# The last chunk of a scan turned inside the next output projection, with its product moved to the end

## The chip, the cores and the metric

One core of one Trainium2 chip runs the whole program. The metric is the device time of one execution in microseconds (us). The kernel before takes 3092.04 us, the median of three runs between 3091.47 and 3092.46. The profiler recorded one further execution of 3090.91 us. Engines are called as the profile calls them: PE is TensorE's matrix multiplication, DVE VectorE, ACT ScalarE, POOL GpSimd, SP SyncE, which issues most transfers.

## The reference

A small decoder trunk of two layers over 2048 tokens of width 1024, in float32: a Mamba-2 layer with a chunked scan, then a layer of latent attention whose keys and values come from the stream after the first layer. The change lies in the first layer, of which this is the core:

```python
proj = h @ w_in
z, xBC, dt_raw = jnp.split(proj, [D_INNER, D_INNER + CONV_DIM], axis=-1)
xBC = jax.nn.silu(causal_depthwise_conv(xBC, conv_w, conv_b))
xs, Bm, Cm = jnp.split(xBC, [D_INNER, D_INNER + SSM_GROUPS * SSM_STATE], axis=-1)
dt = jax.nn.softplus((dt_raw + dt_bias).astype(jnp.float32))
y = ssd_chunked_scan(xh, dt, A, Bm, Cm)            # 4 groups, each 8 heads of 64
y = y + D_skip[:, None] * xh
y = y * jax.nn.silu(z)
y = y * lax.rsqrt(jnp.mean(y * y, axis=-1, keepdims=True) + EPS)   # per group of 512
return (y * g_out) @ w_out
```

## The kernel before, in words

**Tiling.** The 2048 tokens are four blocks b of 512, and the 2048 inner columns four groups g of 512. The pair (b, g) is an item; the sixteen items run in order, b outermost. For an item there are four pieces of work. `xbc` and `zgate` are the input projections, matrix products into PSUM banks of the tag "mm", of which there are four. `zgate` ends with its four row tiles, each bank read by ACT (L639, a tanh) and then by DVE (L640) into the tile sz, after which the bank is free. `ssd` is the scan over four chunks of 128 rows. `outp` is the output projection, in two halves n of 512 output columns. Each half is a `sweep` of 16 products: four row tiles i by four column slices k of the inner dimension. A product is three matmuls (L88, L89, L90), of high and low parts of both operands. When a row tile has its four products, DVE adds the bank to the residual rows hs (L719).

**Between scan and projection.** A finished chunk of the scan, y (128 rows by 512), leaves ACT at L900. The projection needs it with the inner dimension on the partitions, so `turn` transposes it: four PE transposes (L812) into a PSUM bank of the tag "tr" (four banks as well), and from there ACT makes the high part and DVE the low part of a tile yT (L119 and L120, for block 0 L111 and L112). Row tile i of `outp` uses the yT of chunk i. The chunks 0 to 2 are turned in the course of the next chunk; chunk 3 is turned in the last but one of the scan's 20 steps.

**Interleaving.** In item (b, g), the program goes through the 8 parts of `outp` of the item before, then the parts of `xbc` and `zgate` of the item after, and takes a step of the scan of (b, g) whenever its share of the 20 is due (the `while` in `mamba`). In the items with g = 2 three further parts come behind them: loading and normalising the next block's rows, transposing them into xT, and `steps(b + 1)`. The last makes the step sizes of the whole next block: 16 matmuls (L733), a copy by ACT (L737), four transposes (L740), twenty-five short DVE instructions in a chain (L755 to L771, a softplus by series), three matmuls for the sums along a chunk (L773 to L775), and from these ACT's and DVE's tiles d_cum, d_dec, d_ecum and d_wend (L777 to L783). `steps(1)`, for example, is emitted at the end of item (0, 2). The following scan (0, 3) still works on block 0 and needs none of its results, but a scan of a later item does.

**Order.** Nothing here is sorted by hand at the level of instructions: the Tile framework sets each engine's order when the program is built, by priorities and by its own estimates of durations. Each engine then runs its list strictly in that order. So the order that the program is emitted in and the order that an engine runs differ, and a change of the source may move other instructions than those it touches.

**A boundary.** Where one item's scan ends and its `outp` begins, PE has the last matmuls of `zgate` of the next item, L812 of the last chunk, and then `outp`'s products. The first instructions of the scan that follows are L834 and L835 (the transposed B and the product CB), then L850 (four transposes of x) and L870 (the products within a chunk). On ACT and DVE, L844, L841, L845 and L853 belong to the same first steps.

Of the kernel before, what the change touches and what calls it, by code (L numbers as in the profile page):

```python
# [71 lines left out]
class Net:  # L72
# [16 lines left out]
        mm(out, l_hi, r_lo, start=False, stop=False)  # L89
        mm(out, l_lo, r_hi, start=False, stop=stop)  # L90

    def sweep(self, nk, banks, weights, product, evacuate):


        ni, w = len(banks), {}
        order = [(k, i) for i in range(ni) for k in (0, 1)]
        order += [(k, i) for k in range(2, nk - 2) for i in range(ni)]
        order += [(k, i) for i in range(ni) for k in (nk - 2, nk - 1)]
        for n, (k, i) in enumerate(order):
            if k not in w:  # L100
                w[k] = weights(k)
            product(banks[i], k, i, w[k], k == 0, k == nk - 1)
            if k == nk - 1:
                evacuate(banks[i], i)
            if n % ni == ni - 1:
                yield
# [233 lines left out]
    def mamba(self, cp):  # L340
        nc = self.nc
        self.state = [None] * G
        self.xn, self.xT, self.dtv, self.conv, self.sz, self.yT, self.rr, self.hs = {}, {}, {}, {}, {}, {}, {}, {}
        items = [(b, g) for b in range(NB) for g in range(G)]
        self.load_x(0, self.a["x"][0:TB])
        self.layer_constants(cp)
        self.held, self.owed = {}, []
        first = [self.t(self.sp, "big", [P, D], bufs=2) for _ in range(2)]
        first += [self.t(self.hh, "hs", [P, D], bufs=4) for _ in range(4)]
        first += [self.t(self.sp, "yT", [P, D], bufs=4) for _ in range(4)]  # L350

        def later(kind):
            return self.t(self.hh, "hx", [P, D], bufs=4)

        def together(*parts):
            for group in zip_longest(*parts):
                yield

        def beneath(part, *others):
            for _ in part:  # L360
                for other in others:
                    next(other, None)
                yield

        def behind(part, n):
            for _ in range(n):
                yield
            yield from part

        hold = self.scan(0, (0,), lambda kind: first.pop(0), True)  # L370
        rest = [self.scan(0, (kind,), lambda kind: first.pop(0), True) for kind in (1, 2)]
        ahead = self.scan(1, (0, 1, 2), later)
        for part in (hold, self.prep(0, self.g0), rest[0], self.steps(0), together(self.xbc(0, 0), rest[1]),
                     together(self.zgate(0, 0), ahead)):
            for _ in part:
                pass
        def thinned(part, n):
            for m, _ in enumerate(part):
                yield
                if m % n == n - 1:  # L380
                    yield

        background = thinned(self.second_weights(), 2)
        for n, (b, g) in enumerate(items):
            parts, total = [], 0
            if n:
                parts.append(self.outp(*items[n - 1]))
                total += 8
            turned = iter(())
            if g == G - 2:  # L390
                self.load_x(b + 1, self.a["x"][(b + 1) * TB:(b + 2) * TB] if b + 1 < NB else self.h_d[0:TB])
                turned = behind(self.prep(b + 1, self.g0 if b + 1 < NB else None, each=1), 2)
            if n + 1 < len(items):
                beside = iter(())
                if b == 0 and g < 2:
                    beside = self.scan(g + 2, (0, 1, 2), later, early=2)
                elif b == 1:
                    beside = thinned(self.out_power(g), 1)
                elif b:
                    beside = background  # L400
                parts += [beneath(self.xbc(*items[n + 1]), beside), beneath(self.zgate(*items[n + 1]), beside, turned)]
                if b < 2 or (b, g) == (NB - 1, G - 2):
                    parts.append(beside)
                total += 24
            else:
                parts.append(self.mla_gate(0, 0))
                total += 8
            if g == G - 2:
                parts.append(turned)
                total += 2  # L410
                if b + 1 < NB:
                    parts.append(self.steps(b + 1))
                    total += 1
            scan, done, step = self.ssd(b, g), 0, 0
            for part in parts:
                for _ in part:
                    step += 1
                    while done * total < 20 * step and done < 20:
                        next(scan, None)
                        done += 1  # L420
            for _ in scan:
                pass
        self.tail = self.outp(*items[-1])
# [274 lines left out]
    def outp(self, b, g):  # L698

        nc, a, t0 = self.nc, self.a, b * TB  # L700
        if g == 0:
            self.hs[b] = [self.t(self.hh, "hs", [P, D], bufs=4) for _ in range(4)]
            for i in range(4):
                nc.sync.dma_start(self.hs[b][i], a["x"][t0 + i * P:t0 + (i + 1) * P, :])
        hs, yT, rr = self.hs[b], self.yT.pop((b, g)), self.rr.pop((b, g))
        for n in range(2):
            banks = [self.t(self.pp, "mm", [P, TB], bufs=4) for _ in range(4)]

            made = {}

            def weights(j):
                return self.w_out(b, g, n, j, made)

            def product(bank, j, i, w, start, stop):
                self.mm3(bank, yT[i][:, 0, j, :], yT[i][:, 1, j, :], *w, start, stop)

            def evacuate(bank, i):
                hv = hs[i][:, n * 512:(n + 1) * 512]
                nc.vector.scalar_tensor_tensor(hv, bank, rr[:, i:i + 1], hv, ALU.mult, ALU.add)  # L719

            yield from self.sweep(4, banks, weights, product, evacuate)
        if g == G - 1:
            for i in range(4):
                nc.sync.dma_start(self.h_d[t0 + i * P:t0 + (i + 1) * P, :], hs[i])
# [64 lines left out]
    def ssd(self, b, g):  # L789
# [3 lines left out]
        BT, CT, *xs = self.conv.pop((b, g))  # L793
        szs = self.sz.pop((b, g))
        ms, pw = (self.t(self.sm, n, [P, 4]) for n in ("ms", "pw"))
        self.yT[b, g] = []

        def v8(x):
            return x.rearrange("p (h d) -> p h d", h=8)
# [9 lines left out]
        def turn(y):  # L809
            ps = self.t(self.pp, "tr", [P, TB], bufs=4)  # L810
            for j in range(4):
                nc.tensor.transpose(ps[:, j * P:(j + 1) * P], y[:, j * P:(j + 1) * P], self.ident)  # L812
            u = self.t(self.sp, "yT", [P, 2, 4, P], F16 if b else F32R, bufs=4)
            (self.pair16 if b else self.split)(u[:, 0], u[:, 1], ps.rearrange("p (j t) -> p j t", j=4))
            self.yT[b, g].append(u)

        ready = []
        if b:
            old = halves(pair("Sp", TB, 1), self.state[g])
        for c in range(4):  # L820
# [42 lines left out]
            if ready:  # L863
                turn(ready.pop(0))
                yield
# [34 lines left out]
                act(y, y, AF.Copy, scale=pw[:, c:c + 1])  # L900
            yield
            ready.append(y)
        turn(ready.pop(0))
        yield
        r = self.rsqrt(self.sm, ms, 4)
        rr = self.t(self.sm, "rr", [P, 4])
# [613 lines left out]
```

## Time and profile before

| | |
|---|---|
| median of three runs | 3092.04 us |
| the profiled execution | 3090.91 us |
| span from its first to its last instruction | 3088.9 us |
| PE busy | 2995.3 us (97%) |
| DVE busy | 2313.6 us (75%) |
| ACT busy | 1931.2 us (63%) |
| POOL busy | 615.4 us (20%) |
| mean granted PE clock | 0.994 |

The span leaves out 2.0 us of the profiled execution's own time, and the median is 1.1 us above that. The share of busy time is a mean over the whole program, of which the sixteen items are the first half: the last scan step of the items ends at about 1534 us. Names in a row are the program's tile names: `y<-y,pw 128x512` writes 128 partitions by 512 elements of y. A row of the timeline has the start, the duration, the engine, the line, the operation and, in brackets, how long the engine stood idle before it and what released it. Matmuls overlap in the pipeline, so the distance from one start to the next tells the pace, not the duration. A wait that is shown by line and tile is the sum over the program, with the number of times and the longest.

### The profile page before, as it was taken

What the parts mean: (1) busy time and instruction counts of PE and PEld (TensorE: products, weight loads), DVE (VectorE), ACT (ScalarE), POOL (GpSimd) and SP (SyncE); (2) the same over time, 40 slices, a digit from 0 to 9 for tenths busy, and PEclk for the clock granted to TensorE, in tenths of its full rate; (3) what the DMA queues carried; (4) which work ended last, traced back from release to release, by engine and by line L of the source; (5) the groups of instructions that cost most, each with busy time, mean ns of one, the idle gap of its engine ahead of it and who ended that gap; (6) DMA issues with size and microseconds to landing.
All of it is one profiled execution on the core that took longest, in us unless ns stands there. A gap on an engine that the chain in (4) does not pass through costs nothing.

```text
span 3088.9 us, 51063 instructions
## 1 busy us (share of the span) xinstructions
PE 2995.3 (97%) x17758; PEld 1760.5 (57%) x17758; DVE 2313.6 (75%) x5034; ACT 1931.2 (63%) x4920; POOL 615.4 (20%) x842
## 2 busy tenths in 40 slices
PE   7899999999999999999999999999999999999998
PEld 3466655545455554545555455466666666665777
DVE  6789887778777787887755544488888888888676
ACT  8777566655666665565534333278888888888522
POOL 0212122211212112222111211422222222222100
PEclk9999999999999999999999999999999999999999
DMA  8675436354455366354466555622323223232494
GB/s 287 225 242 184 146 105 218 127 169 152 147 203 163 131 194 217 133 195 150 147 206 205 184 184 163 195 67 53 68 54 66 53 54 65 54 87 76 126 270 153
DMA packets 205064, 457.09 MB, mean 148 GB/s; under 512 B 28115, under 2 KB 57555, under 8 KB 203365
## 3 DMA queue, kind: packets, MB, share of 16 engines
q1 hardware_dynamic: 176948, 375.94, 38.0%
q0 software_dynamic: 27856, 77.89, 9.8%
q8 instruction: 140, 2.29, 0.3%
q14 instruction: 120, 0.97, 0.1%
HBM read 340.99 MB, written 112.73 MB: 147 GB/s over the span
## 4 chain that ended last, share of the span: by engine, by line
PE 36%; ACT 6%; DVE 6%; issue 4%; DMA 2%; POOL 0%; SPq 0%; ACTq 0%; POOLq 0%; DVEq 0%
PE mm L88 6%; PE mm L90 6%; PE mm L89 6%; PE tr L1254 5%; PE tr L88 3%; ACT Pr L1236 3%; PE tr L89 3%; PE tr L90 3%; PE tr L1264 2%; PE tr L1265 2%; ACT PTs L119 2%; DVE PTs L120 1%; DVE mx L1228 1%; DMA os<-ri_d 1%; DMA wr<-in_mla_w_out_dram 0%
## 5 line engine op out<-in xcount | busy, mean ns | idle before, releaser
L120 DVE SCALAR_TENSOR_TENSOR PTs<-tr,PTs 128x512 f16<-128x512 f32 (+3 forms) x640 | 376.8, 607 | 99.2 <-ACT PTs L119 92.7
L1236 ACT ACTIVATE Pr<-mm,nm 128x512 f32<-128x512 f32 (+2 forms) x631 | 397.5, 638 | 21.7 <-DVE nm L1231 21.5
L119 ACT ACTIVATE PTs<-tr 128x512 f16<-128x512 f32 (+3 forms) x640 | 331.3, 541 | 121.0 <-PE tr L1254 111.5
L1228 DVE TENSOR_REDUCE mx<-mm 128x1 f32<-128x512 f32 (+2 forms) x569 | 338.9, 617 | 31.4 <-PE mm L90 26.7
L1254 PE MATMUL tr<-pack,Pr 128*128 128x128 f32 x2176 | 320.4, 273 | 3.4 <-DVE PTs L120 2.4
L88 PE MATMUL mm<-xT,wsp 128*128 128x512 f16 x800 | 305.7, 382 | 7.6 <-ACT wsp L119 4.6
L89 PE MATMUL mm<-xT,wsp 128*128 128x512 f16 x800 | 304.9, 381 | 0.0
L90 PE MATMUL mm<-xT,wsp 128*128 128x512 f16 x800 | 304.5, 381 | 0.0
L1254 PEld LDWEIGHTS tr<-pack,Pr 128*128 128x128 f32 x2176 | 253.3, 141 | 76.0 <-PE mm L1223 6.7
L88 PE MATMUL mm<-K,xT 96*128 96x512 f16 (+2 forms) x639 | 222.5, 348 | 16.8 <-ACT Pr L1236 14.1
L88 PE MATMUL mm<-wsp,xT 128*128 128x512 f16 (+1 forms) x640 | 232.2, 364 | 4.5 <-ACT craw L610 4.3
L89 PE MATMUL mm<-wsp,xT 128*128 128x512 f16 (+1 forms) x640 | 232.3, 363 | 3.2 <-DVE wsp L120 3.2
L616 DVE SCALAR_TENSOR_TENSOR cacc<-craw,pack,cacc 128x512 f32<-128x512 f32 x288 | 219.5, 791 | 17.6 <-ACT cacc L614 17.0
L90 PE MATMUL mm<-wsp,xT 128*128 128x512 f16 (+1 forms) x640 | 232.1, 363 | 0.0
L89 PEld LDWEIGHTS <-xT 128*128 128x128 f16 (+1 forms) x1408 | 138.1, 98 | 152.1 <-issue 43.2
L1264 PE MATMUL tr<-PTs,xT 128*128 128x512 f16 (+3 forms) x640 | 221.0, 347 | 1.7 <-ACT Os L1271 1.3
L90 PE MATMUL mm<-K,xT 96*128 96x512 f16 (+2 forms) x639 | 221.8, 347 | 0.0
L89 PE MATMUL mm<-K,xT 96*128 96x512 f16 (+2 forms) x639 | 221.2, 346 | 0.0
L1265 PE MATMUL tr<-PTs,xT 128*128 128x512 f16 (+3 forms) x640 | 219.2, 347 | 0.0
L90 PEld LDWEIGHTS <-xT 128*128 128x128 f16 (+1 forms) x1408 | 137.0, 97 | 133.1 <-issue 5.5
L88 PEld LDWEIGHTS <-xT 128*128 128x128 f16 (+1 forms) x1408 | 137.6, 98 | 120.1 <-issue 8.5
L88 PE MATMUL mm<-wsp,yT 128*128 128x512 f16 (+1 forms) x512 | 197.4, 385 | 1.2 <-DVE sz L640 1.0
(458 smaller groups left out, 6796.0 us busy)
## 6 DMA issues: line engine op xcount, KB each, us to landing
wsp<-wi_d SPq DMA_DIRECT2D x96, 512.0 KB, 3.7
big<-cumT SPq DMA_DIRECT2D x64, 512.0 KB, 4.8
wraw<-in_ssm_w_out_dram SPq DMA_DIRECT2D x96, 256.0 KB, 3.8
wi_d<-wsp SPq DMA_DIRECT2D x32, 512.0 KB, 3.6
wsp<-wo_d SPq DMA_DIRECT2D x32, 512.0 KB, 3.4
wsp<-wu_d SPq DMA_DIRECT2D x28, 512.0 KB, 3.8
hx<-in_ssm_w_in_dram SPq DMA_DIRECT2D x48, 256.0 KB, 4.4
wraw<-in_ssm_w_in_dram SPq DMA_DIRECT2D x48, 256.0 KB, 4.5
```

Of the source, the lines that this page charges most:

```text
L88: mm(out, l_hi, r_hi, start=start, stop=False)
L89: mm(out, l_hi, r_lo, start=False, stop=False)
L90: mm(out, l_lo, r_hi, start=False, stop=stop)
L119: self.nc.scalar.activation(hi, src, AF.Copy, scale=scale)
L120: self.nc.vector.scalar_tensor_tensor(lo, src, scale, hi, ALU.mult, ALU.subtract)
L616: nc.vector.scalar_tensor_tensor(acc, raw[:, k:k + TB], wk[k], acc, ALU.mult, ALU.add)
L1228: v.tensor_reduce(mx[:, n:n + 1], s[:, :w], AX.X, ALU.max)
L1236: nc.scalar.activation(x[:, :w], s[:, :w], AF.Exp, bias=nm, accum_out=sm[:, j, n:n + 1])
L1254: nc.tensor.transpose(pt[:, j * P:(j + 1) * P], st["P"][j][kb], self.ident)
L1264: nc.tensor.matmul(st["O"][:, c], vals[h][:, kb, :], u[:, 0], start=kb == 0, stop=False)
L1265: nc.tensor.matmul(st["O"][:, c], vals[h][:, kb, :], u[:, 1], start=False, stop=kb == nk - 1)
```

## The change

The last chunk's `turn` is no longer a step of the scan. It is kept in a table `last_turn` and called by `outp`, once, after the first part of its first half: in the order of emission behind four products and behind the next scan's first step. So that the projection has work that does not need the last row tile, the first half's sweep orders its sixteen products differently: those of the row tiles 0 to 2 first, twelve of them, then the four of row tile 3. The second half keeps its order. No instruction is added or removed, and the values are the same.

```diff
-    def sweep(self, nk, banks, weights, product, evacuate):
+    def sweep(self, nk, banks, weights, product, evacuate, waits=False):
...
         order += [(k, i) for i in range(ni) for k in (nk - 2, nk - 1)]
+        if waits:
+            order = [x for x in order if x[1] < ni - 1] + [x for x in order if x[1] == ni - 1]
         for n, (k, i) in enumerate(order):
...
         self.state = [None] * G
+        self.last_turn = {}
...
-            yield from self.sweep(4, banks, weights, product, evacuate)
+            for m, _ in enumerate(self.sweep(4, banks, weights, product, evacuate, n == 0)):
+                yield
+                if n + m == 0:
+                    self.last_turn.pop((b, g))()
...
-        self.yT[b, g] = []
+        rows = self.yT[b, g] = []
...
-            self.yT[b, g].append(u)
+            rows.append(u)
...
-        turn(ready.pop(0))
+        self.last_turn[b, g] = lambda: turn(ready.pop(0))
         yield
```

The lines of the changed file stand a few further down: L812 is L818, L719 is L722, L733 L739, L740 L746, L771 L777, L773 L779, L834 L840, L850 L856, L870 L876, L845 L851, L853 L859, L112 and L120 are L114 and L122, L640 is L643.

PE at the end of item (1, 3), an ordinary boundary (xT are the operands of `zgate`, yT those of `outp`). Before:

```order
L90 LDWEIGHTS xT_8103
L90 MATMUL mm_8957<-wsp_9131,xT_8103 128x512
L812 MATMUL tr_9151<-pack,y_9000 128x128 x4
L88 LDWEIGHTS xT_8095
L88 MATMUL mm_8958<-wsp_9131,xT_8095 128x512
```

Of the change:

```order
L90 LDWEIGHTS yT_8752
L90 MATMUL mm_9197<-wsp_9200,yT_8752 128x512
L840 MATMUL tr_9228<-pack,BC_8637 128x128
L841 MATMUL tr_9228<-BC_8682,BC_8637 128x128
L818 MATMUL tr_9249<-pack,y_9000 128x128 x4
L88 LDWEIGHTS yT_9037
L88 MATMUL mm_9198<-wsp_9200,yT_9037 128x512
```

The turn stood between two products of `zgate`, with twelve more matmuls of `zgate` behind it before the first of `outp`; it now stands behind the first twelve matmuls of `outp` and the first two of the next scan.

PE in the item (1, 2), where `steps(2)` lies (d_... and big_8131 or big_8123 are its tiles). Before, up to the sums along a chunk:

```order
L90 LDWEIGHTS yT_7655
L90 MATMUL mm_8374<-wsp_8377,yT_7655 128x512
L773 MATMUL tr_8166<-big_8131,pack 128x128
L774 MATMUL tr_8166<-big_8131,ones 128x128
L775 MATMUL tr_8166<-pack,big_8131 128x128
L834 MATMUL tr_8242<-pack,BC_7500 128x128
L835 MATMUL tr_8242<-BC_7532,BC_7500 128x128
L850 MATMUL tr_8275<-pack,xs_7737 128x128
```

Of the change:

```order
L90 LDWEIGHTS yT_7974
L90 MATMUL mm_8204<-wsp_8269,yT_7974 128x512
L779 MATMUL tr_8158<-big_8123,pack 128x128
L780 MATMUL tr_8158<-big_8123,ones 128x128
L781 MATMUL tr_8158<-pack,big_8123 128x128
L840 MATMUL tr_8234<-pack,BC_7500 128x128
L841 MATMUL tr_8234<-BC_7532,BC_7500 128x128
L818 MATMUL tr_8255<-pack,y_7907 128x128 x4
L856 MATMUL tr_8286<-pack,xs_7737 128x128
```

The three matmuls L773 to L775 stood in the second half of `outp` (bank mm_8374); they now stand behind the last product of row tile 2 in the first half (bank mm_8204), with L812 behind them. Between the transposes L740 and the first of the three, PE's list has 55, 50 and 64 matmuls in the items (0, 2), (1, 2) and (2, 2) before, and 31, 30 and 30 of the change.

DVE at the same place, the instructions that make the low part of the last chunk's yT. Before, between two other turns:

```order
L120 SCALAR_TENSOR_TENSOR xT_8103<-tr_8098,pack,xT_8103 128x512
L120 SCALAR_TENSOR_TENSOR yT_8111<-tr_8106,yT_8111 128x512
L242 TENSOR_SCALAR rsy_8187<-rsb_8185 128x4
```

Of the change:

```order
L777 TENSOR_TENSOR big_8123<-d_dt_8155,pack 128x128
L786 TENSOR_TENSOR d_wend_8165<-tr_8158,d_cum_8162 128x128
L789 COPY big_8123<-tr_8158 128x128
L114 TENSOR_TENSOR Bt_8237<-tr_8234,Bt_8237 128x128
L788 TENSOR_TENSOR d_wend_8165<-d_wend_8165,d_dt_8155 128x128
L847 TENSOR_TENSOR CB_8243<-tr_8234,pack 128x128
L851 TENSOR_TENSOR big_8232<-big_8232,CB_8243 128x1024
L859 TENSOR_TENSOR Xd_8291<-tr_8286,d_dt_4074 128x512
L122 SCALAR_TENSOR_TENSOR yT_8260<-tr_8255,yT_8260 128x512
```

The low part was made ahead of the steps' chain; it now comes behind the whole chain and behind the first instructions of the next scan (CB, the 128x1024 product, Xd).

## The prediction

> **What bounds the kernel now.** I read the page's busy table first: PE works 2995.3 of 3088.9 us, so a change that leaves PE's instructions alone can move only the 94 us in which it stands, and the time that a lower clock costs it. Then I read what PE waits for at the lines that the change touches.
>
> ```profile
> PE tr L812 <- ACT y L900: 9.8, 7, 3.2
> PE tr L812 <- ACT xT L119: 1.9, 1, 1.9
> PE tr L773 <- DVE big L771: 1.2, 2, 0.7
> PE mm L88 <- DVE sz L640: 1.0, 3, 0.5
> PE tr L812 <- DVE hx L552: 0.9, 1, 0.9
> PE tr L812 <- DVE xT L120: 0.5, 1, 0.5
> ```
>
> The columns are the sum in us, the number of times and the longest. L812 waits 13.1 us in all: 9.8 for the chunk's own y, and 3.3 at the three boundaries beside which the next block's steps lie, for a "tr" bank. That is all that this change can take away directly. L773, in the chain of the steps, and the first matmul of a bank (L88, for sz) wait almost nothing.
>
> Next the granted clock around the wait of the item (1, 1), by windows; the columns are the window, its length, busy time and count of PE, its loads, DVE, ACT and POOL, then the clock, the DMA share and GB/s.
>
> ```profile
> 626.28 0.84 PE L812 MATMUL tr<-pack,y 128*128 128x128 f32 x4 [1.96 <-ACT y L900]
> ```
> ```profile
> 624.30:626.60 2.30, 0.34 (x4) 0.32 (x4) 2.06 (x14) 2.30 (x6) 0.00 (x0) 1.00 0.87 314
> 626.60:630.00 3.40, 3.40 (x12) 1.42 (x10) 2.57 (x13) 3.40 (x8) 0.00 (x0) 0.50 0.75 254
> 630.00:634.00 4.00, 4.00 (x22) 2.01 (x21) 3.90 (x13) 3.36 (x5) 0.00 (x0) 1.00 0.22 68
> ```
>
> After a wait of 1.96 us PE runs 3.4 us at clock 0.50: that doubles its work there, so about 1.7 us are lost behind the wait. The trace has five such stretches behind L812's waits, so up to 13.1 + 8.5 = 21.6 us hang on this instruction. The question is what stands in its place.
>
> **Part 1, an ordinary boundary.** PE's new list has outp's first products where L812 stood. They need a "mm" bank, which is free when DVE has read the last of it into sz (L640), behind ACT's L639. The boundary at (1, 3):
>
> ```profile
> 820.91 0.38 PE L90 MATMUL mm<-wsp,xT 128*128 128x512 f16 x1
> 824.47 1.05 PE L812 MATMUL tr<-pack,y 128*128 128x128 f32 x4 [3.18 <-ACT y L900]
> 825.55 1.24 ACT L639 ACTIVATE sz<-mm,half 128x512 f32<-128x512 f32 x2
> 826.64 0.68 DVE L640 SCALAR_TENSOR_TENSOR sz<-sz,mm 128x512 f32<-128x512 f32 x1
> ```
>
> ACT's list has L639 behind L900, in both orders. Without L812, PE goes on at 820.91 + 0.22 with the last twelve matmuls of zgate at 0.216 each (the pace is worked out in part 2) and reaches outp's first at 823.7. The bank is free at 826.64 + 0.68 = 827.3, and 0.1 later the matmul starts: a wait of 3.7 in place of 3.18. The same working for three others:
>
> ```profile
> 535.76 0.66 PE L812 MATMUL tr<-pack,y 128*128 128x128 f32 x4 [1.34 <-ACT y L900]
> 1195.34 0.66 PE L812 MATMUL tr<-pack,y 128*128 128x128 f32 x4 [2.41 <-ACT y L900]
> ```
> ```profile
> 537.93 0.68 DVE L640 SCALAR_TENSOR_TENSOR sz<-sz,mm 128x512 f32<-128x512 f32 x1
> 629.14 0.68 DVE L640 SCALAR_TENSOR_TENSOR sz<-sz,mm 128x512 f32<-128x512 f32 x1
> 1198.36 0.68 DVE L640 SCALAR_TENSOR_TENSOR sz<-sz,mm 128x512 f32<-128x512 f32 x1
> ```
>
> PE is there at 535.76 - 1.34 + 2.6 = 537.0, 626.9 and 1195.5; the bank is free at 538.7, 629.9 and 1199.1. The waits are 1.7, 3.0 and 3.6 where 1.34, 1.96 and 2.41 stood. The four sum to 12.0 against 8.9: **+3.1**, and the stretches at half clock behind them stay as many. Before, L812's wait covered this one. The rest of L812's 9.8 (0.9, at later boundaries) I let go: **-0.6**. The price lies between -8.9 (the bank is free earlier than the rows say) and +4. That row tile 3 is late costs nothing here: its product stands at least 24 matmuls, 5.2 us, behind its turn, and ACT and DVE need 0.7 us each for yT.
>
> **Part 2, the three boundaries with the next block's steps.** The reorder lets twelve products of outp run early, and the scheduler, which holds the steps' chain to be short, puts L773 to L775 right behind them: 31, 30 and 30 matmuls behind L740 where 55, 50 and 64 stood. L773 needs the end of DVE's chain, and everything on PE queues behind it: the next scan's L834, L835, L812 itself, and the rest of outp. How long the chain takes at (1, 2):
>
> ```profile
> 735.02 0.39 PE L89 MATMUL mm<-wsp,yT 128*128 128x512 f16 x1
> 745.61 0.38 PE L90 MATMUL mm<-wsp,yT 128*128 128x512 f16 x1
> 746.51 0.46 PE L773 MATMUL tr<-big,pack 128*128 128x128 f32 x2 [0.52 <-DVE big L771]
> 748.02 0.38 PE L88 MATMUL mm<-wsp,yT 128*128 128x512 f16 x1
> ```
> ```profile
> 735.13 0.29 DVE L755 TENSOR_TENSOR big<-tr,pack 128x128 f32<-128x128 f32 x1 [3.06 <-PE tr L740]
> 746.07 0.29 DVE L771 TENSOR_TENSOR big<-d_dt,pack 128x128 f32<-128x128 f32 x1
> 749.60 1.22 DVE L845 TENSOR_TENSOR big<-big,CB 128x1024 f32<-128x1024 f32 x1
> ```
>
> The first two rows are the first and last of the 50 matmuls: 49 gaps in 10.59 us, 0.216 each. DVE's chain runs from 735.13 to 746.36, 11.23 us; of the change it holds three evictions of hs where it held four, each 0.66 from start to start like the next fence's conversion: 10.6. L755 starts 0.11 behind the first matmul and L773 0.15 behind the chain's end, so L773 can start 10.9 us after that matmul. PE is there after 30 x 0.216 = 6.5: it waits **4.3** (before, 0.52). At (0, 2) and (2, 2):
>
> ```profile
> 358.73 0.50 PE L88 MATMUL mm<-wsp,yT 128*128 128x512 f32 x1
> 371.11 0.39 PE L88 MATMUL mm<-wsp,yT 128*128 128x512 f32 x1
> ```
> ```profile
> 358.84 0.29 DVE L755 TENSOR_TENSOR big<-tr,pack 128x128 f32<-128x128 f32 x1 [2.17 <-PE tr L740]
> 370.33 0.74 DVE L115 SCALAR_TENSOR_TENSOR wsp<-wraw,pack,wsp 128x512 fp32r<-128x512 f32 x1
> 370.99 0.28 DVE L771 TENSOR_TENSOR big<-d_dt,pack 128x128 f32<-128x128 f32 x1
> ```
> ```profile
> 1104.73 0.29 DVE L755 TENSOR_TENSOR big<-tr,pack 128x128 f32<-128x128 f32 x1 [0.23 <-PE tr L740]
> 1118.12 0.28 DVE L771 TENSOR_TENSOR big<-d_dt,pack 128x128 f32<-128x128 f32 x1
> ```
>
> At (0, 2) the chain takes 12.43, of the change less one eviction and two conversions, 10.5; PE needs 31 x 0.229 = 7.1: a wait of **3.6**. At (2, 2) it takes 13.68, less an eviction and one conversion, 12.35; PE needs 6.5: **6.1**. Together 14.0, less the 0.5 of before: **+13.5**. Bounds: 0.7 for each conversion or eviction that moves, so 11 to 15. L812's 3.3 us here are no gain, since the bank they wait for is now taken by L733, next in the list.
>
> **Part 3, row tile 3 at those boundaries.** The turn comes behind L773, and DVE's half of yT behind the big product L845 and Xd. At (1, 2) L845 ends at 750.82, 4.3 us after L773's start; 0.7 for yT makes 5.0. PE, from L773 to the end of L850, takes 748.02 - 746.51 = 1.5, with 0.44 for L812, seven matmuls (1.5) and nine of L870 (0.3) 3.8 until it needs the low part: a wait of **1.3**, and the same at (0, 2). At (2, 2) ACT has a weight conversion ahead of its half, but a wait of before falls away:
>
> ```profile
> 1119.36 0.72 ACT L119 ACTIVATE wraw<-wraw,gains 128x512 f16<-128x512 f32 x1 [1.95 <-DMA wraw<-in_mla_w_in_dram]
> 1126.10 1.12 PE L870 MATMUL tr<-Xd,big 128*64 128x64 f32 x31 [2.21 <-issue]
> ```
>
> With the conversion 1.3 + 0.7, and up to 4.0 if its transfer is late again; less 2.21, between -0.9 and +4. I take 0. **+2.6** in all.
>
> **Part 4, the clock.** Waits of 1.96 us were followed by one half-clock stretch; three new waits of 3.6 to 6.1 bring one or two each. Four at 1.7 are 6.8; what PE waits in part 3 it would have waited anyway, which covers about 2.3: **+4.5**, between 2.5 and 8.5.
>
> [...]
>
> **Part 5, what is paid back.** Behind the new waits PE has 20 to 34 more matmuls (4.3 to 7.3 us) between L773 and the item's end than before, so the next boundary's wait, at (1, 3) and (2, 3), may shrink. Against it, (1, 0) and (1, 1) wait there too without any steps ahead of them: that wait comes from the chain behind the last chunk. I take **-3**, between 0 and -10.7 (3.7 + 3.6 and two stretches).
>
> **The sum:** 3.1 - 0.6 + 13.5 + 2.6 + 4.5 - 3 = +20.1 on the profiled 3090.9, that is 3111.0; the median lies 1.1 above the profiled execution: **3112 us**. With all costs low and the payback whole it is +7 or so, 3099; with all high, +33, 3125.
>
> **The rivals.** *ACT's list at (2, 3)*, on the far side of the forecast: two conversions of the value weights (L477) now stand ahead of L639.
>
> ```profile
> 1208.74 0.72 ACT L477 ACTIVATE wraw<-wraw,pack 128x512 fp32r<-128x512 f32 x1 [0.67 <-DMA wraw<-in_kv_w_up_dram]
> ```
>
> If their transfer lands as late as it did, tanh waits until 1209.5 where it started about 1197.6; PE lags by up to 8 us by then, so 4 to 12 more: 3116 to 3124. For it: the row's wait for a DMA. Against it: the transfers are issued earlier in the new order. 0.15.
>
> *The banks are free in time* at ordinary boundaries, so that L812's 8.9 us and three stretches (5.1) are gained there, while parts 2 to 4 stand: 20.1 - 2.5 - 14 = +3.6, 3096. Against it, L639 is behind L900 in ACT's list. 0.12.
>
> *Faster:* the wait at L812 is the true bound and L773 finds its chain done. It decides if DVE's chain falls below the 6.5 us that PE needs; then the 13.1 us and five stretches go, less what sz takes: 3070 to 3085. Against it, 10.6 us of instructions in one engine's list. 0.09.
>
> *Nothing measurable:* the payback is whole and the banks are free earlier by a microsecond or two: 3092 to 3098. 0.10.
>
> **The numbers.** The forecast has 0.54, within 3099 to 3125. The range 3094 to 3125 takes in the rivals at 3096 and 3116 to 3124. A measurement tells 0.2%, 6.2 us, from no change. Slower: the forecast, the first rival and some of the second, 0.77; the same: most of the second and the last, 0.13; faster: 0.10.
>
> **What would show it.** Right: PE waits of 4 to 6 us at L773 (now L779) in three places, for DVE's big; L812 (now L818) waits below 1 us in all, while the wait of L88 for sz rises from 1.0 to about 12; clock 0.50 behind the three. Wrong: L88's wait for sz stays small (part 1), L779 waits under 2 us (part 2), or the end waits of (1, 3) and (2, 3) vanish (part 5 was the larger).

## The result, and the profile after

The changed kernel takes 3110.12 us, the median of six runs from 3106.36 to 3120.19; the kernel before, run beside it, 3092.06 us. The ratio is 1.007, with a 95% interval from 1.0059 to 1.0081: slower by 18 to 25 us. The forecast was 3112 us, slower. The profiled execution took 3106.36 us with a span of 3104.4, that is 15.5 more than the span before, and PE is busy 2998.4 us where it was 2995.3. It was the fastest of the six, so an account of this trace explains 15.5 us and leaves the rest of the 18 to 25 open.

What PE waits for in the items of the first layer (the waits between 300 and 1600 us; the columns are the sum, the times and the longest), in the changed kernel:

```profile
PE tr L779 <- DVE big L777: 15.1, 3, 7.2
PE mm L88 <- DVE sz L643: 10.9, 7, 3.6
PE mm L88 <- ACT craw L613: 8.4, 5, 3.3
PE tr L739 <- DVE xT L122: 2.9, 2, 1.8
PE tr L739 <- DVE hx L555: 0.9, 1, 0.9
PE mm L88 <- ACT yT L121: 0.8, 1, 0.8
```

The same view of the kernel before, where it has more than the prediction showed:

```profile
PE mm L88 <- ACT craw L610: 5.9, 4, 3.3
PE tr L870 <- issue: 2.2, 1, 2.2
PE tr L89 <- POOL Xp L806: 1.8, 3, 0.6
PE mm L88 <- DVE hs L719: 1.4, 2, 0.9
PE tr L773 <- DVE big L771: 0.5, 1, 0.5
```

Read the two side by side. The turn (L818) no longer waits at all. The 13.1 us that it waited before are at other instructions: 10.9 at the first matmuls of outp, for sz, and 3.8 at L739 (2.9 + 0.9), which now takes the "tr" bank that the turn took. On top stand 15.1 us at L779, the sums along a chunk of the next block's steps, where 0.5 stood. The three waits of L779, by the timeline of PE:

```profile
372.05 0.46 PE L779 MATMUL tr<-big,pack 128*128 128x128 f32 x2 [3.64 <-DVE big L777]
748.75 0.46 PE L779 MATMUL tr<-big,pack 128*128 128x128 f32 x1 [4.31 <-DVE big L777]
1123.12 0.77 PE L779 MATMUL tr<-big,pack 128*128 128x128 f32 x2 [7.15 <-DVE big L777]
```

They were forecast as 3.6, 4.3 and 6.1. The granted clock around four waits of the changed kernel, by windows (the third number from the right is the clock):

```profile
634.00:638.00 4.00, 2.20 (x11) 0.88 (x9) 3.76 (x20) 4.00 (x8) 0.00 (x0) 1.00 0.96 322
834.00:838.00 4.00, 3.80 (x22) 2.16 (x22) 3.64 (x13) 1.10 (x3) 0.00 (x0) 1.00 0.84 238
1123.00:1130.00 7.00, 6.13 (x27) 4.49 (x27) 4.43 (x10) 3.66 (x10) 0.00 (x0) 0.66 0.80 252
1216.00:1220.00 4.00, 3.94 (x11) 1.49 (x11) 1.80 (x4) 1.03 (x2) 0.00 (x0) 0.57 0.00 0
```

Behind the waits for sz at (1, 1) and (1, 3), 1.80 and 1.86 us long, the clock stays at 1.00; behind the one at (2, 3), 3.62 us long, it falls, and at L779 at (2, 2) it is at 0.50 for two stretches, from 1120.9 to 1127.7 us. Counted in narrow windows up to 1620 us, the trace of before has nine stretches of 3.4 us at half clock and the changed one eleven. In such a stretch the matmuls start 0.43 us apart (before, from 627.34 to 629.48 us) and after it 0.22 (from 630.18 us on), so half of the time that PE worked in the stretches is taken as lost: by this estimate 14.0 us before and 16.4 now, +2.4.

The account by these views: L779 +14.6 (15.1 - 0.5); sz and the turn's y together +0.6 (10.9 - 0.5 - 9.8); craw +2.5; the bank before the steps +0.5 (3.8 - 3.3); row tile 3 and the wait in its place -1.4 (0.8 - 2.2); Xp and hs, for which PE no longer waits, -3.2 (1.8 + 1.4); the clock +2.4. That is +16.0 against 15.5 of the span; small waits that the views above leave out, and those of the second layer, are not in it.

### The profile page after: what moved, and what is told of

The parts are those of the page before. It is cut to its first block, busy times and chain, and to the rows that moved or that the text cites. A ratio compares the mean times of both kernels' runs of the same rounds, so it can differ in the third digit from the quotient of the medians.

```text
span 3104.4 us, 51077 instructions
## 1 busy us (share of the span) xinstructions
PE 2998.4 (97%) x17758; PEld 1763.8 (57%) x17758; DVE 2315.5 (75%) x5034; ACT 1930.9 (62%) x4920; POOL 614.9 (20%) x842
## 4 chain that ended last, share of the span: by engine, by line
PE 57%; DVE 14%; ACT 9%; DMA 5%; issue 5%; POOL 1%; SPq 0%; ACTq 0%; DVEq 0%; POOLq 0%
PE mm L88 12%; PE mm L90 11%; PE mm L89 11%; PE tr L1260 5%; PE tr L88 3%; PE tr L90 3%; PE tr L89 3%; DVE cacc L619 3%; ACT Pr L1242 3%; PE tr L1270 2%; PE tr L1271 2%; ACT PTs L121 2%; PE tr L876 1%; DMA big<-cumT 1%; DVE PTs L122 1%
## 5 line engine op out<-in xcount | busy, mean ns | idle before, releaser
L122 DVE SCALAR_TENSOR_TENSOR PTs<-tr,PTs 128x512 f16<-128x512 f32 (+3 forms) x640 | 376.9, 607 | 98.2 <-ACT PTs L121 91.8
L88 PE MATMUL mm<-K,xT 96*128 96x512 f16 (+2 forms) x639 | 222.5, 348 | 16.4 <-ACT Pr L1242 13.5
L88 PE MATMUL mm<-wsp,yT 128*128 128x512 f16 (+1 forms) x512 | 198.4, 388 | 12.3 <-DVE sz L643 11.5
```

The costliest lines, as they stand in the source:

```text
L88: mm(out, l_hi, r_hi, start=start, stop=False)
L122: self.nc.vector.scalar_tensor_tensor(lo, src, scale, hi, ALU.mult, ALU.subtract)
```

## Experiments

Theory A says that the three boundaries with the next block's steps carry the loss, since L779 stands too early there. Rival B says that the ordinary boundaries carry it, by outp's wait for sz. Under A two causes are open: that the turn is emitted behind the steps (A1), or that the reorder lets outp's products run ahead (A2, as the prediction had it). Executions of one kernel differ by up to 0.6% (those of before ran from 3080 to 3098 us), so the verdicts rest on ratios to runs of before on the same chip.

### The change at the three boundaries alone, and everywhere else alone

```diff
-            for m, _ in enumerate(self.sweep(4, banks, weights, product, evacuate, n == 0)):
+            for m, _ in enumerate(self.sweep(4, banks, weights, product, evacuate, n == 0 and (g == 2 and b < 3))):
...
-                if n + m == 0:
+                if n + m == 0 and (g == 2 and b < 3):
...
-        self.last_turn[b, g] = lambda: turn(ready.pop(0))
+        if (g == 2 and b < 3):
+            self.last_turn[b, g] = lambda: turn(ready.pop(0))
+        else:
+            turn(ready.pop(0))
```

The second kernel has `not (g == 2 and b < 3)` in the three places.

> The change at the three boundaries with the next block's steps alone, (0, 2), (1, 2) and (2, 2). PE's list there has L779 behind 31, 30 and 30 matmuls, as in the changed kernel. Theory A (these three boundaries carry the loss): PE waits at L779 of about 3.6, 4.3 and 7 us, and a time 10 to 17 us above before, 3102 to 3109. Rival B (the ordinary boundaries carry it, by outp's first matmul waiting for sz): within 3 us of before, 3089 to 3095.

> The change everywhere but at those three boundaries. Theory A: no wait at L779; at the ordinary boundaries the wait at the turn (8.9 us at four of them before) is replaced by one for sz of about the same size; 3086 to 3096. Rival B: 3102 to 3110.

The three boundaries alone: 3108.1 us, ratio 1.0064 (1.0052 to 1.0077), that is 16 to 24 us above before where theory A said 10 to 17. Everywhere else alone: 3093.6 us, ratio 1.0019 (1.001 to 1.0029). The waits of the first and of the second kernel, between 300 and 1600 us:

```profile
PE tr L779 <- DVE big L777: 15.5, 3, 7.5
PE tr L818 <- ACT y L906: 8.7, 5, 2.7
PE mm L88 <- DVE sz L643: 1.5, 3, 0.9
```
```profile
PE mm L88 <- DVE sz L643: 11.6, 7, 3.8
PE tr L779 <- DVE big L777: 0.6, 1, 0.6
PE tr L818 <- ACT y L906: 0.3, 1, 0.3
```

Each part of the change makes its own wait and leaves the other alone. The first carries about 0.64 of the 0.70%, the second about 0.19; the two add up to a little more than the whole, within their intervals. Theory A holds. B is wrong as the main cause and right as a small one: at the ordinary boundaries a wait of 8.7 to 9.8 us for y is given for one of 11.6 for sz, and the time rises by 3 to 9 us.

### The reorder alone, and the turn alone

The first keeps the new order of the products and turns the last chunk in the scan; the second moves the turn and keeps the old order.

```diff
# reorder alone
-                if n + m == 0:
-                    self.last_turn.pop((b, g))()
...
-        self.last_turn[b, g] = lambda: turn(ready.pop(0))
+        turn(ready.pop(0))
# turn alone
-            for m, _ in enumerate(self.sweep(4, banks, weights, product, evacuate, n == 0)):
+            for m, _ in enumerate(self.sweep(4, banks, weights, product, evacuate)):
```

> Only the order of the products: row tile 3 comes last in the first half, but the last chunk is turned in the scan as before. PE's list has the sums along a chunk behind 55, 50 and 61 matmuls (before: 55, 50, 64). Theory A1 (where the turn is emitted brings them forward, not the reorder): their wait stays under 1 us each and the time within 4 us of before, 3088 to 3096. Rival A2, as the prediction had it (the reorder itself lets them come early): waits of 3.6 to 6 us there and 3102 to 3110.

> Only the turn is moved; the products keep the order of before. PE's list has L779 behind 31, 30 and 30 matmuls again. Theory A1: waits at L779 of 3.6, 4.3 and 7 us as in the changed kernel, and 3103 to 3112. Rival A2: L779 finds its operand, and what is lost is a wait for the last row tile at each boundary, since its first products stand early in the emitted order: some 1 to 3 us at each of 15 boundaries, 3110 to 3130.

The reorder alone: 3092.18 us, ratio 1.0009 (1.0000 to 1.0018). The turn alone: 3122.3 us, ratio 1.0106 (1.0092 to 1.0120). The waits of the one and of the other (in the first, the sums are L777 and their operand L775, the turn L816):

```profile
PE tr L816 <- ACT y L904: 7.8, 6, 2.4
PE tr L777 <- DVE big L775: 2.5, 2, 1.4
```
```profile
PE tr L779 <- DVE big L777: 15.1, 3, 7.2
PE mm L88 <- DVE sz L643: 13.2, 7, 4.2
PE mm L90 <- DVE yT L122: 4.3, 3, 1.7
PE mm L88 <- ACT yT L121: 3.8, 3, 1.6
```

A2 falls. With the reorder alone the sums stay far back, behind 55, 50 and 61 matmuls, and wait 2.5 us in all; the longest wait, 1.4 us, is a little more than the 1 us that A1 allowed. With the turn alone they come forward to the same 31, 30 and 30 matmuls and wait the same 15.1 us. So it is where the turn is emitted that moves L779. The reorder has the use that it seems to have: without it, PE waits 8.1 us for the last row tile (4.3 + 3.8) where the whole change has 0.8, and 13.2 us for sz instead of 10.9. So the turn alone is slower than the whole change. Its time, 3122.3 us, lies above what A1 expected, since A1 left this out, and within what A2 expected; it is the waits at L779, which A2 denied, that decide against A2.

### The sums along a chunk emitted later

If the turn's place behind the steps is the cause, it must help to emit the steps' second part behind the turn. `steps` yields ahead of its product with ea, and outp runs the rest after its first half.

```diff
+        yield
         v.tensor_tensor(v4(dA), v4(dt), b4(self.ea), ALU.mult)
...
-                    parts.append(self.steps(b + 1))
+                    self.sums[b, g] = self.steps(b + 1)
+                    parts.append(islice(self.sums[b, g], 1))
...
+            if n == 0:
+                for _ in self.sums.pop((b, g), ()):
+                    pass
```

> The change, and the second part of the steps (from the product with ea on: the three matmuls and what follows from them) is emitted after outp's first half instead of before outp. PE's list has the three matmuls behind 58, 57 and 57 matmuls. Theory A1 (the turn was emitted behind these matmuls and so they came forward): their waits fall below 1 us each, the half clock behind them goes, and the time comes back to that of the change without these three boundaries, 3088 to 3097. Rival: at these boundaries the late turn itself costs, since row tile 3 waits for DVE behind the next scan's first step; then waits of 1 to 4 us for yT remain and the time is 3099 to 3106.

> The kernel before, with the same second part of the steps emitted after outp's first half: the control to the run above. PE's list has the three matmuls behind 53, 56 and 65 matmuls (before: 55, 50, 64). Theory A1: nothing to gain, since they waited 0.5 us in all; within 4 us of before. Rival (it is emission after outp's first half that saves time in itself): 4 to 15 us below before.

With the change: 3086.99 us, ratio 0.9995 (0.9986 to 1.0004). Without it: 3084.45 us, ratio 0.9983 (0.9975 to 0.9992). The waits of the change with late sums (the sums are L784):

```profile
PE mm L88 <- DVE sz L644: 8.2, 7, 2.6
PE tr L784 <- DVE big L782: 1.3, 2, 0.9
PE mm L90 <- DVE yT L122: 0.5, 1, 0.5
```

The whole loss is gone, 15.1 us at L779 having become 1.3, and row tile 3 waits 0.5 in all; the time came out 1 us below the range of A1. A1 stands, and the rival (that the late turn costs by itself at these boundaries) does not. The control came out at the edge of what was expected of it: the late sums take 2 to 8 us off the kernel before by the interval, which theory A1 does not explain. Its trace has neither the 2.2 us at L870 nor the 1.8 us for Xp that the kernel before waits, and the y of the last chunk costs 8.5 us where it cost 9.8; what in the new order does this no run here takes apart. Beside this control, the change with its late sums is still no gain.

### The banks of outp made free earlier

The second cost is outp's first matmul, waiting for sz behind L906 in ACT's list. In this pair zgate's sweep takes its last four column slices row tile by row tile, so that its first bank is finished earlier (`tail` is a new argument of `sweep`, 2 everywhere else); the first kernel has the change at the ordinary boundaries, the second is the kernel before.

```diff
-        order += [(k, i) for k in range(2, nk - 2) for i in range(ni)]
-        order += [(k, i) for i in range(ni) for k in (nk - 2, nk - 1)]
+        order += [(k, i) for k in range(2, nk - tail) for i in range(ni)]
+        order += [(k, i) for i in range(ni) for k in range(nk - tail, nk)]
...
-        yield from self.sweep(KD, banks, weights, product, evacuate)
+        yield from self.sweep(KD, banks, weights, product, evacuate, tail=4)
```

> The change at the ordinary boundaries alone, and zgate's sweep takes the last four column slices, not the last two, row tile by row tile, so that its first row tile is finished 36 matmuls before the end instead of 18. ACT's list then has the first one or two tanh of sz ahead of the last chunk's L906. Theory S (outp's first matmul waits for sz, which stands behind L906): the waits for sz of 1.8, 1.9, 2.6 and 3.8 us fall below 1 us each, and the time is 3078 to 3088. Rival: something else is late there too, outp's weights (four of five buffers are held by zgate) or the second row tile's sz, and PE waits for those: 3089 to 3100.

> The kernel before with the same zgate sweep: the control. Theory S: L812's wait for the chunk's y stays (9.8 us), and the time stays within 4 us of before. Rival (the early banks alone bring it): 5 us or more below before.

The change at the ordinary boundaries with early banks: 3084.05 us, ratio 0.9986 (0.9977 to 0.9996), where it was 1.0019 without them. The kernel before with early banks: 3090.91 us, ratio 1.0006 (0.9997 to 1.0014). Waits of the first and of the second:

```profile
PE mm L88 <- DVE sz L643: 2.0, 4, 1.0
PE mm L90 <- DVE yT L122: 1.0, 2, 0.7
PE tr L818 <- ACT y L906: 0.5, 1, 0.5
```
```profile
PE tr L812 <- ACT y L900: 10.5, 6, 3.5
```

And ACT at the boundary (1, 3), first without the early banks (the change at the ordinary boundaries alone), then with them:

```profile
824.06 0.72 ACT L906 ACTIVATE y<-y,pw 128x512 f32<-128x512 f32 x1 [1.52 <-DVE rsy L244]
824.69 1.32 ACT L121 ACTIVATE wsp<-wraw,gou 128x512 f16<-128x512 f32 x2
825.92 2.39 ACT L642 ACTIVATE sz<-mm,half 128x512 f32<-128x512 f32 x4
```
```profile
822.65 0.72 ACT L906 ACTIVATE y<-y,pw 128x512 f32<-128x512 f32 x1 [1.49 <-DVE rsy L244]
823.27 0.67 ACT L642 ACTIVATE sz<-mm,half 128x512 f32<-128x512 f32 x1
826.22 1.06 ACT L850 ACTIVATE big<-big 128x1024 f32<-128x1024 f32 x1 [2.28 <-DVE big L849]
```

Without them all four tanh stand behind L906 and two weight conversions; with them only one is left behind it, right behind. The wait for sz falls from 11.6 to 2.0 us, and neither the early banks alone nor the late turn alone gains: each leaves the other's wait in place.

### All three together

The change at every boundary, with late sums and early banks; and the same with the change at the ordinary boundaries alone.

> The change at every boundary, with the steps' second part after outp's first half and with zgate's last four column slices row tile by row tile. If the three parts add up (the change and the late sums: 1.3 us below before; the early banks took 9.5 us off the change at the ordinary boundaries): no wait over 1 us at the three matmuls of the sums or for sz, and 3074 to 3082. If the late turn costs at the boundaries with the steps, or the early banks only help where the turn is late, less: 3082 to 3088.

> As the run above, but with the change at the ordinary boundaries alone: at the three boundaries with the steps the last chunk is turned in the scan. If the late turn does nothing at those three (the waits there are for a bank that is late either way, 3.2 us with or without it): within 2 us of the run above. If it gains there: 2 to 5 us slower than it; if it costs there: 2 to 5 us faster.

They take 3080.9 us, ratio 0.9981 (0.9972 to 0.9990), and 3081.65 us, ratio 0.9978 (0.9970 to 0.9987). The waits of the first that belong to the change:

```profile
PE tr L784 <- DVE big L782: 1.2, 2, 0.9
PE mm L90 <- DVE yT L122: 0.7, 1, 0.7
PE mm L88 <- DVE sz L644: 0.2, 1, 0.2
```

The two are equal within their intervals: at the three boundaries with the steps the late turn neither gains nor costs once the sums are out of its way, as PE waits for the "tr" bank there either way: 3.3 us at L743 in the first kernel, 3.4 at the turn in the second, by the sums of their rows for xT. Both beat the kernel before and the changed one. They don't clearly beat the kernel before with late sums alone (0.9983): the waits of PE at these instructions are down to about 2 us, yet the time follows only in part.

## Why the prediction was right, and where it was not

**The direction, the time and the main term were right.** Part 2 forecast 14.0 us of waits at L779 and 15.1 were measured, by the rule it gave: the length of DVE's chain less the matmuls that stand ahead. At (0, 2) and (1, 2) it was right to a tenth, and so were its two sides: DVE's chain ran 10.71 and 10.69 us where 10.5 and 10.6 stood. At (2, 2) the chain was said to shrink from 13.68 to 12.35 us by two instructions less; it ran 13.55:

```profile
1109.42 0.29 DVE L761 TENSOR_TENSOR big<-tr,pack 128x128 f32<-128x128 f32 x1
1114.25 0.29 DVE L849 TENSOR_SCALAR big<-big,d_cum 128x128 f32<-128x128 f32 x1 [0.53 <-DMA big<-cumT]
1122.69 0.28 DVE L777 TENSOR_TENSOR big<-d_dt,pack 128x128 f32<-128x128 f32 x1
```

The work that left the chain left gaps that it had filled, among them 0.53 us for the transfer of cumT.

**The cause given for part 2 was wrong.** "The reorder lets twelve products of outp run early, and the scheduler ... puts L773 to L775 right behind them": the reorder alone leaves them where they were, and the turn alone moves them. The list on which the term rested was right, the reason for it was not. What in the framework ties the sums to a turn that is emitted behind them is open; that emitting them behind the turn undoes it is shown.

**Part 1 was right in kind.** The turn's wait was exchanged for one for sz: where "about 12" was forecast, 11.5 were measured in the whole program, 10.9 of them between 300 and 1600 us. Of the four that were worked out, (1, 0) and (2, 3) came at 1.93 and 3.62 where 1.7 and 3.6 stood; (1, 1) and (1, 3) at 1.80 and 1.86 where 3.0 and 3.7 stood. The rows for these two, from ACT of the changed kernel and from DVE of the kernel before:

```profile
830.53 0.72 ACT L906 ACTIVATE y<-y,pw 128x512 f32<-128x512 f32 x1 [1.53 <-DVE rsy L244]
```
```profile
627.63 0.28 DVE L843 TENSOR_SCALAR big<-big,d_cum 128x128 f32<-128x128 f32 x1 [0.80 <-DMA big<-cumT]
```

At (1, 3), PE waits from 834.20 - 1.86 = 832.34, and would have come to the turn's old place twelve matmuls (2.6 us) sooner, at 829.7; y is ready at 831.25, 1.5 us later, where it was 3.18 later before. Only a part of this is the payback of part 5, as the two kernels of the first experiment show at the same boundary, the change everywhere but at the steps and the change at the steps alone:

```profile
827.73 0.38 PE L88 MATMUL mm<-wsp,yT 128*128 128x512 f16 x1 [2.58 <-DVE sz L643]
```
```profile
837.81 0.48 PE L818 MATMUL tr<-pack,y 128*128 128x128 f32 x1 [2.67 <-ACT y L906]
```

With hardly a wait at the steps ahead of it, sz already costs 2.58 there and not 3.7: 1.1 us are an error of part 1, whose cause these rows do not show. The wait at the steps then takes off 0.7 (2.58 to 1.86), or 0.5 if the turn is where it was (3.18 to 2.67). At (2, 3) it takes off 0.1 to 0.2 (3.77 to 3.62 for sz, 2.41 to 2.30 at the turn). So part 5, -3, was about -0.6 to -0.9 in waits. At (1, 1), DVE waited 0.80 us for the transfer of cumT ahead of L640 before, and does not now.

**Part 4 and part 3 were mis-sized.** The three waits at L779 brought four stretches at half clock, as said. But two behind the wait for the bank at (1, 2) and two behind the turn's waits at (1, 1) and (1, 3) did not come again, and two came at about 219 and 1373 us, behind waits that the change hardly touched: +2.4 in all where +4.5 stood, with more going and coming than the term held. Part 3's +2.6 was -1.4: at half clock (at (1, 2) from 748.8 to 752.3 us) PE came to row tile 3 so late that DVE was done (there it needed the low part 6.1 us behind L779's start, where 3.8 stood), and only 0.76 us at (2, 2) was left, while the 2.21 of before fell away.

**A term was missed.** At (2, 3) PE waits 3.33 us for craw, which no part had. In ACT's list two background weight conversions come ahead of L613 there, and each waited for a transfer:

```profile
1183.36 0.61 ACT L121 ACTIVATE wraw<-wraw,gains 128x384 f16<-128x384 f32 x1 [0.70 <-DMA wraw<-in_mla_w_in_dram]
1184.92 0.61 ACT L121 ACTIVATE wraw<-wraw,gains 128x384 f16<-128x384 f32 x1 [0.95 <-DMA wq_d<-wraw]
```
```profile
1187.17 0.38 PE L88 MATMUL mm<-wsp,xT 128*128 128x512 f16 x1 [3.33 <-ACT craw L613]
```

The prediction's first rival looked for such a wait at L639 behind L477 (now L480), some 25 us later in ACT's list; there the second conversion waited 0.33 us for its transfer, and the tanh starts 3.23 us behind the start of L906, where it started 2.99 behind that of L900 before:

```profile
1213.05 0.72 ACT L480 ACTIVATE wraw<-wraw,pack 128x512 fp32r<-128x512 f32 x1 [0.33 <-DMA wraw<-in_kv_w_up_dram]
```

**The time was met by luck.** The sum on the profiled execution was +20.1, and the account found +16.0 there: part 2 was +14.6 where +13.5 stood, parts 1 and 5 together +0.6 where -0.5 stood, part 3 -1.4 where +2.6 stood, part 4 +2.4 where +4.5 stood, and what no part held (craw, the bank, Xp and hs) -0.2. That the median came within 2 us of the forecast all the same is owed to the profiled execution, which lies 3.8 us below the median where the forecast reckoned with 1.1; on the trace it was 4.6 us off. The low end, +7, leaves part 1 at +3.1; with part 1's own bound of -8.9 the bounds of the parts add up to about -5, a case that the prediction has only as its second rival.

## What to carry to other kernels

Where a framework sets each engine's order, moving a piece of work past another in the source can move the other one too: read the compiled order at every place where the moved piece meets a long chain, and compare the chain's length with the work that now stands ahead of its consumer. A wait that is taken from one instruction can go to the next resource that the same late engine frees: here y (9.8 us of waits before) and sz (10.9 after) both came from ACT's list, and at the ordinary boundaries only changing both gained (ratio 0.9986, against 1.0019 and 1.0006 for one alone). And test the two halves of a change apart, since the half that looks responsible may not be.

## What the runs showed of the hardware

**The clock did not follow the length of a wait alone.** A wait of 1.96 us at (1, 1) was followed by 3.4 us at half clock before, and one of 1.80 at the same place of the changed kernel by none; waits of 1.93 and 1.86 us were followed by none, one of 3.62 by one; at one of 7.15 there are two, the first from 2.2 us before its end; and the wait of 3.33 us for craw at (2, 3) by none. How the wait lies on a grid agrees better with them: in the traces of before and after every stretch at one clock, but for the last of each, lasts a multiple of 3.41 us (3.41 and 6.83 at 0.50; 6.83, 17.07, 58.03 and more at 1.00), so these traces can be laid out in windows of 3.41 us, and PE's idle time counted in each. The 1.96 us lie in one window, behind which the clock falls to 0.50; the 3.33 us are divided between two, behind which it stays at 1.00 (the number behind the comma is PE's busy time; kernel before, whose next row is the prediction's 626.60:630.00 at clock 0.50, then the changed one):

```profile
623.20:626.60 3.40, 1.44 (x9) 0.61 (x7) 3.16 (x18) 3.40 (x8) 0.00 (x0) 1.00 0.84 298
```
```profile
1182.34:1185.75 3.41, 1.49 (x7) 0.58 (x6) 2.85 (x10) 1.77 (x4) 1.06 (x1) 1.00 0.54 175
1185.76:1189.17 3.41, 2.00 (x9) 0.87 (x9) 1.92 (x5) 3.38 (x6) 0.37 (x2) 1.00 0.84 290
```

Each of the 18 windows of these two traces at full clock behind which it fell has at least 1.76 us in which PE stood; none of the 1,761 others has more than 1.96. So here the clock was 0.50 in the 3.41 us behind every window at full clock in which PE stood for more than 1.96 us, and between 1.76 and 1.96 us it went either way. This is counted from PE's rows, whose ends are modelled, and no run here varies it on purpose. It also fits the stretches that came and went in part 4: the windows lie elsewhere in each trace (the first stretch at 0.50 starts 29.3 us into the span before and 28.6 us into it after), and the wait for craw of 3.28 us at 1352 us before lies across two windows (1.6 and 1.7, clock 1.00 behind both), that of 2.55 us at 1370 us of the changed kernel in one, with clock 0.50 behind it.
